# A masked softmax bound by its transfers: the cuts of the stores of batches 6 to 12

## The chip, the cores and the metric

The kernel runs on one core of a Trainium2 chip. The metric is the device time of one execution in microseconds (us); a smaller one is better. Most runs of one kernel agree within about 0.3%. "Faster" or "slower" means by more than 2%. Batches, loads and stores are numbered from 0, so "store 6" writes batch 6, the seventh.

## The reference

```python
x: float32 [16, 8, 256, 256]        # batch, heads, seq_q, seq_k
lengths: int32 [16], each in 128..255
for b in range(16):
    m = x[b, :, :, :lengths[b]]
    e = exp(m - max(m, axis=-1))
    result[b, :, :, :lengths[b]] = e / sum(e, axis=-1)      # the rest of result is 0
```

A batch is 2048 rows of 256 numbers, 2.10 MB. The inputs are drawn with a fixed seed, so the lengths, and with them the bytes that the loads bring, are the same in every run. A load has landed when the engine that waits for it sees all of it arrived, shortly after its last packet. A hole is a stretch in which the DMA engines have too little to do.

## The kernel before

A batch lies in SBUF as 128 partitions of 16 rows (`nt` = 16), each partition 16 KB and contiguous in memory too. There are eight slots. Loads 0 to 3 go out on SyncE's queue; loads 4 to 15 on GpSimd's, each only as wide as its batch's length needs. VectorE masks (one instruction a batch), ScalarE takes exponentials and row sums, VectorE divides (two halves a batch); SyncE stores. The cuts of the stores are in `parts`:

```python
def parts(b):
    if b == 0:
        cuts = [0, nt]
    elif b < 10:
        cuts = [0, half, half + quarter, nt]
    elif b < 12 or b == batch - 1:
        cuts = [0, half, nt]
    else:
        cuts = [0, nt]
    return [slice(i, j) for i, j in zip(cuts, cuts[1:])]
...
# SyncE: the stores
for b in range(batch):
    s_b = s_st[b % 2]
    for s in parts(b):
        nc.sync.wait_ge(s_out, 2 * b + (s.stop - 1) // half + 1)    # the divisions that it needs
        if b >= 2 and s.start == 0:
            nc.sync.wait_ge(s_b, 64 * (b // 2 + 1))                 # store b-2 has landed
        nc.sync.dma_start(out=out_f[b, :, s, :], in_=xt[:, b % slots, s, :]).then_inc(...)
...
# GpSimd: load n waits for load n-2 and for store n-8
# VectorE: the order of its work
for b in range(batch):
    ...
    mask(b + 1); divide(b, 0); divide(b, 1)
```

At most two batches' stores, and two loads, are in flight. A part that ends in the first half needs one division, a whole store needs both. And batch b is divided only after the mask of batch b+1, so it waits for load b+1.

The softmax here doesn't subtract the row's maximum and nothing guards it: scores larger than these inputs give would overflow.

Of the kernel before, what the change touches and what calls it, by code (L numbers as in the profile page):

```python
# [20 lines left out]
def kernel(  # L21
# [9 lines left out]
    batch, heads, seq_q, seq_k = x.shape  # L31
# [18 lines left out]
    def parts(b):  # L50


        if b == 0:
            cuts = [0, nt]
        elif b < 10:
            cuts = [0, half, half + quarter, nt]
        elif b < 12 or b == batch - 1:
            cuts = [0, half, nt]
        else:
            cuts = [0, nt]  # L60
        return [slice(i, j) for i, j in zip(cuts, cuts[1:])]
# [17 lines left out]
    with tc.tile_critical(no_gpsimd_drain=True):  # L79
# [32 lines left out]
# [3 lines that stand above are left out]
                nc.sync.wait_ge(s_out, 2 * b + (s.stop - 1) // half + 1)  # L115
                if b >= 2 and s.start == 0:
                    nc.sync.wait_ge(s_b, 64 * (b // 2 + 1))
                nc.sync.dma_start(  # L118
                    out=out_f[b, :, s, :], in_=xt[:, b % slots, s, :]
                ).then_inc(s_b, 16 * ((s.stop - s.start) // quarter))  # L120
# [162 lines left out]
```

## Time and profile before

The kernel before takes 156.7 us (156.70 to 157.01 in four runs). Its profiled execution took 156.32 us, with a span of 154.7.

| what | before | how it is read |
|---|---|---|
| bytes moved | 62.08 MB | page, DMA queues; the change leaves it as it is |
| DMA share, 24 to 139.5 us | 1.01 to 1.02 | by stretch; the DMA share is the mean busy share of the 16 DMA engines, and about 1.01 is what full engines show in these records |
| mask 14, mask 15 start | 120.01, 127.35 | VectorE in order of time; mask 14 starts when its load has landed; mask 15 when its load has (127.14) and VectorE has ended its division (127.24) |
| last division ends | 139.46 | the same |
| last packet of a store ends | 152.8 | packet records |

The lines themselves stand in the prediction.

### The profile page before, as it was taken

The numbers are of one execution on the slowest core, as the hardware profiler recorded it, in microseconds if no ns is written. First come the engines' busy times: TensorE is split into PE (matmuls) and PEld (weight loads), VectorE is DVE, ScalarE is ACT, GpSimd is POOL, SyncE is SP. The second block draws the span as 40 slices with busy tenths as digits, with TensorE's granted clock in tenths as the row PEclk, the third lists the DMA queues.
The fourth block names the chain that finished last, engine by engine and source line by source line (L and its number), as shares of the span: only waits on it lengthen the run. The fifth ranks groups of instructions, "written<-read, shape, count | busy, mean of one in ns | idle before, by whom it ended". The sixth has DMA issues, their size and how long they took to land.

```text
span 154.7 us, 1317 instructions
## 1 busy us (share of the span) xinstructions
PE 0.2 (0%) x1; PEld 0.1 (0%) x1; DVE 115.1 (74%) x84; ACT 105.2 (68%) x514; POOL 19.0 (12%) x25
## 2 busy tenths in 40 slices
PE   0000000000000000000000000000000000000000
PEld 0000000000000000000000000000000000000000
DVE  1249999952999994966979499999894999990000
ACT  3087799992698997591978849798969297920000
POOL 4910031000320200202020020202000000000000
DMA  4999999999999999999999999999999999999993
GB/s 108 430 445 424 436 309 416 409 411 436 423 404 388 423 405 416 412 412 422 398 421 412 411 413 404 414 409 412 417 409 450 417 420 426 443 432 436 424 415 144
DMA packets 10132, 62.08 MB, mean 401 GB/s; under 512 B 866, under 2 KB 962, under 8 KB 6802
## 3 DMA queue, kind: packets, MB, share of 16 engines
q1 hardware_dynamic: 6048, 41.95, 66.1%
q0 software_dynamic: 4080, 20.12, 32.1%
q14 instruction: 2, 0.02, 0.0%
q10 hardware_dynamic: 2, 0.00, 0.0%
HBM read 28.51 MB, written 33.55 MB: 401 GB/s over the span
## 4 chain that ended last, share of the span: by engine, by line
DMA 71%; DVE 12%; issue 4%; POOLq 1%; SPq 1%; DVEq 0%
DMA xt<-in_x_dram 60%; DMA out_dram<-xt 11%; DVE xt L222 9%; DVE xt L195 3%; SPq L109 1%; POOLq L135 1%; DVE inv_sum L219 0%; POOLq L130 0%; SPq L111 0%; SPq L118 0%; POOLq L157 0%; POOLq L159 0%; DVEq L212 0%; POOLq L137 0%; SPq L278 0%
## 5 line engine op out<-in xcount | busy, mean ns | idle before, releaser
L249 ACT ACTIVATE xt<-xt x256 | 102.4, 402 | 29.6 <-DVE xt L195 29.6
L222 DVE TENSOR_TENSOR xt<-xt,inv_sum 128x2048 f32<-128x2048 f32 x32 | 73.3, 2292 | 1.1
L195 DVE SCALAR_TENSOR_TENSOR xt<-down,len_s,xt 128x2048 f32<-128x2048 f32 (+1 forms) x17 | 37.8, 2224 | 19.8 <-DMA xt<-in_x_dram 19.4
L249 ACT ACTIVATION_READ_ACCUMULATOR xt<-xt x256 | 48.1, 188 | 0.0
L130 POOL DMA_DIRECT2D xt<-in_x_dram x12 | 12.8, 1066 | 91.3 <-DMA out_dram<-xt 62.8
L219 DVE RECIPROCAL inv_sum<-row_sum 128x8 f32<-128x8 f32 x32 | 6.3, 196 | 1.2 <-ACT xt L249 1.2
L149 POOL MEMSET xt<- 128x1536 f32 x4 | 5.3, 1387 | 1.1 <-DVE len_s L186 1.1
L241 ACT ACT_TABLE_LOAD x1 | 1.3, 1283 | 1.6 <-SPq L79 1.6
L178 DVE TENSOR_SCALAR down<-iota_i 128x256 f32<-128x256 int32 x1 | 0.3, 299 | 1.6 <-POOL iota_i L141 1.6
L183 DVE CAST len_b<-word 1x16 bf16<-1x16 int32 x1 | 0.2, 162 | 0.4 <-DMA word<-in_lengths_dram 0.4
L186 DVE TENSOR_SCALAR len_s<-len_f 128x16 f32<-128x16 f32 x1 | 0.2, 175 | 0.3 <-PE len_f L165 0.3
L141 POOL IOTA iota_i<- 128x256 int32 x1 | 0.3, 332 | 0.6 <-SPq L79 0.6
L146 POOL MEMSET seed<- 1x1 f32 x2 | 0.3, 164 | 0.0
L241 ACT ACTIVATE warm<-const-float32-0.0 128x1 f32<-128x1 f32 x1 | 0.2, 203 | 0.0
L144 POOL MEMSET ones<- 1x128 bf16 x1 | 0.2, 197 | 0.0
L165 PE MATMUL len_f<-len_b,ones 1*128 1x16 bf16 x1 | 0.2, 164 | 2.6 <-DVE len_b L183 2.6
L267 POOL MEMSET const-float32-0.0<- 128x1 f32 x1 | 0.1, 99 | 0.3 <-issue 0.3
L165 PEld LDWEIGHTS len_f<-len_b,ones 1*128 1x128 bf16 x1 | 0.1, 99 | 2.6 <-POOL ones L144 2.6
L267 POOL MEMSET const-float32-1.0<- 128x1 f32 x1 | 0.1, 99 | 0.0
L267 POOL MEMSET const-bfloat16-1.0<- 128x1 bf16 x1 | 0.1, 99 | 0.0
L267 POOL MEMSET const-uint8-127<- 128x1 uint8 x1 | 0.1, 99 | 0.0
L267 POOL BASE_LOAD x1 | 0.0, 17 | 0.1
## 6 DMA issues: line engine op xcount, KB each, us to landing
out_dram<-xt SPq DMA_DIRECT2D x15, 1024.0 KB
out_dram<-xt SPq DMA_DIRECT2D x18, 512.0 KB
out_dram<-xt SPq DMA_DIRECT2D x4, 2048.0 KB
xt<-in_x_dram SPq DMA_DIRECT2D x3, 2048.0 KB, 16.1
xt<-in_x_dram POOLq DMA_DIRECT2D x3, 1728.0 KB, 15.9
xt<-in_x_dram POOLq DMA_DIRECT2D x2, 2048.0 KB, 17.5
xt<-in_x_dram POOLq DMA_DIRECT2D x2, 1600.0 KB, 15.1
xt<-in_x_dram POOLq DMA_DIRECT2D x2, 1280.0 KB, 14.2
```

What stands on the lines that cost most here:

```text
L109: nc.sync.dma_start(out=xt[:, 0, s], in_=x_f[0, :, s]).then_inc(s_ld[h], 16)
L130: nc.gpsimd.dma_start(out=xt[:, slot, :, :w], in_=x_n[:, n, :, :w]).then_inc(s_sw[par], 16)
L135: with nc.gpsimd.If(v <= ws[m]):
L141: nc.gpsimd.iota(iota_i, pattern=[[1, seq_k]], base=0, channel_multiplier=0).then_inc(s_iota, 1)
L149: nc.gpsimd.memset(xt[:, b, :, low:], 0.0).then_inc(s_fill, 1)
L165: nc.tensor.matmul(len_f, lhsT=ones, rhs=len_b, start=True, stop=True).then_inc(s_lenf, 1)
L195: return nc.vector.scalar_tensor_tensor(out=t, in0=down[:, None, lo:hi].to_broadcast([P, s.stop - s.start, hi - lo]), scalar=len_s[:, b : ...
L219: step(nc.vector.reciprocal(out=inv_sum[:, b, s], in_=row_sum[:, b, s]))
L222: nc.vector.tensor_tensor(out=t, in0=t, in1=inv_sum[:, b, s, None].to_broadcast([P, half, seq_k]), op=ALU.mult,).then_inc(s_out, 1)
L241: nc.scalar.activation(out=warm, in_=nc.const_aps.tensor(0.0, (P, 1), F32), func=EXP)
L249: ins = nc.scalar.activation(out=e, in_=e, func=EXP, accum_out=sum_h[:, bass.ds(i, 1), j])
L267: nc = _bacc.Bacc("TRN2", target_bir_lowering=False, num_devices=1)
```

## The change

The intent is fewer and larger store transfers (37 become 34) in the part of the run where loads and stores share the engines, with the compute left as it is.

```diff
-        elif b < 10:
+        elif b < 6:
             cuts = [0, half, half + quarter, nt]
-        elif b < 12 or b == batch - 1:
+        elif b < 13 or b == batch - 1:
             cuts = [0, half, nt]
```

Stores 6 to 9 change from a half and two quarters to two halves, store 12 from whole to two halves. The others keep their cuts.

## The prediction

> **What bounds the kernel now.** I read the page from the top, then the stretches by engine, the chain, the waits of SyncE's queue, and the DMA queues stretch by stretch. Batches are numbered from 0. The page of the kernel before says:
>
> ```profile
> span 154.7 us, 1317 instructions
> PE 0.2 (0%) x1; PEld 0.1 (0%) x1; DVE 115.1 (74%) x84; ACT 105.2 (68%) x514; POOL 19.0 (12%) x25
> DMA  4999999999999999999999999999999999999993
> GB/s 108 430 445 424 436 309 416 409 411 436 423 404 388 423 405 416 412 412 422 398 421 412 411 413 404 414 409 412 417 409 450 417 420 426 443 432 436 424 415 144
> DMA 71%; DVE 12%; issue 4%; POOLq 1%; SPq 1%; DVEq 0%
> ```
>
> No compute engine is full, while the DMA engines are over 90% busy in 38 of 40 slices. The chain is 71% DMA. The 62.08 MB that the page counts at about 420 GB/s make nearly the whole span. So only three things can move the time: bytes, cost per byte, or a moment in which the DMA engines have nothing to do. The stretches (last columns: DMA share, GB/s) show that there is none until the stores are drained:
>
> ```profile
> 24.00:80.00 56.00, 0.00 (x0) 0.00 (x0) 45.62 (x32) 44.16 (x220) 5.91 (x6) 1.00 1.01 413
> 80.00:127.10 47.10, 0.00 (x0) 0.00 (x0) 41.88 (x30) 37.08 (x185) 5.17 (x5) 1.00 1.02 416
> 127.10:139.50 12.40, 0.00 (x0) 0.00 (x0) 12.11 (x10) 8.51 (x43) 0.00 (x0) 1.00 1.02 435
> ```
>
> The last piece of the chain and the waits of SyncE's queue from 80 us on show that compute is not what ends the kernel:
>
> ```profile
> 137.17 2.29 DVE xt L222
> ```
>
> ```profile
> SPq L117 <- DMA out_dram<-xt: 62.3, 9, 8.9
> SPq L122 <- DMA out_dram<-xt: 8.2, 1, 8.2
> ...
> SPq L118 <- DVE xt L222: 0.4, 1, 0.4
> ```
>
> The last division ends at 139.5, 15 us ahead of the end; stores wait for stores (at most two batches' stores are in flight), hardly ever for data. Loads too are two deep: the chain is a row of loads, each issued when the one before the last has landed. So both queues always hold work, and how they share the engines depends on the size of their packets. The records of single packets show a whole store as packets of 16384 B, a half as 8192, a quarter as 4096; the loads' packets are 4320 to 4800 B (loads 5 and 15: 16384).
>
> The share is seen by asking for the queues of single stretches (q1 stores, q0 loads; MB; share). Store 6's half, 80.0 to 84.1:
>
> ```profile
> q1 hardware_dynamic: 154, 1.03, 60.6%
> q0 software_dynamic: 156, 0.67, 40.8%
> ```
>
> Its two quarters, 84.1 to 89.4:
>
> ```profile
> q0 software_dynamic: 276, 1.11, 52.5%
> q1 hardware_dynamic: 277, 1.06, 49.7%
> ```
>
> As many packets pass on either side (154 and 156; 277 and 276). For 1.05 MB stored, loads get 0.67 MB beside a half and 1.11 MB beside two quarters.
>
> **What the Trainium skill says.** "DMA: Bandwidth & Descriptors", section "Queues, rings and completion order", says that each DMA engine takes turns between the queues that have work, a packet at a time. The equal counts above agree. The same page, "Bandwidth", gives a fabric ceiling of 435 GB/s; the stretch after the last load moves 435 by the view, and 431 over whole stores by packet times, so stores alone run at it. "VectorE: DVE Perf Modes" gives 2291 ns for an fp32 tensor_tensor of 2048 elements; the row of the division shows 2292, so the compute of the tail won't change.
>
> **The change, part by part.** Stores 1 to 5 keep their cuts. Stores 6 to 9 turn their two quarters into a half; 10 and 11 were halves already; 12 goes from whole to two halves. 13 and 14 stay whole, 15 stays halves. Nothing differs before store 6's second half, at 84.1.
>
> (a) Cost of packets. 8 quarters of 128 packets go (1024 packets of 4096 B, 162.9 ns each by the packet records) and one whole store (128 of 631 ns); 6 halves come (768 of 316.4 ns). −166.9 − 80.8 + 243.0 = −4.7 us of engine time, over 16 engines −0.3 us. Six issues at some 0.45 us fewer on SyncE's queue: off the path, because it mostly waits.
>
> (b) Share of the loads. Six windows at the first halves of stores 4 to 9 gave loads of 0.70, 0.68, 0.67, 0.70, 0.58 and 0.58 MB; mean 0.65 (the low ones hold the end of a load). No second half runs beside these small packets in the trace; single quarters took 0.555 each, with one turn more for each store's closing packet, so I choose 0.59. A store batch of two halves then carries 2.10 + 1.24 = 3.34 MB, at 416 GB/s 8.04 us. Before it carried about 1.8 MB of loads in 9.5 us (79.95 to 89.51 by the packets): close to the mean load of 20.12/12 = 1.68 MB, one load for one store. After, stores run ahead of the loads.
>
> (c) Where loads end. From 80.0 to 127.1 the load queue moves 9.40 MB (the queue's line for that stretch), 2.10 of it load 15, so 7.30 MB are left up to load 14. That takes 7.30/1.24 = 5.89 store batches of 8.04 us: load 14 drains at 127.3 instead of 119.1. Load 15 has big packets and beats halves two to one; it took 7.3 us (119.1 to 126.4) beside some 1.1 MB of stores. After: until 134.6 instead of 126.4, 8 us later.
>
> (d) What stores are left then. At 127.3 store 11 lacks 0.11 of a batch, 0.24 MB. By 134.6, 1.1 MB more are out, so store 12 has 2.10 − 0.86 = 1.24 MB left: 2.9 us at 431 GB/s, until 137.5.
>
> (e) When later stores are ready. VectorE starts a mask about 1.2 us after a load's last packet (14: 0.9, 13: 1.4, 12: 1.3) and ends that turn's second division 7.2 us after (127.35 to 134.58 in the tail: 2.35 + twice 2.45). Mask 14 at 128.5, store 13 ready at 135.7, its packets 1.0 to 1.1 us after the issue (the first load: 1.14 to 2.15), 136.8: in time for 137.5. Store 13 drains 4.87 us later, at 142.4. Mask 15 starts at 135.7 (load 15 and VectorE are both there), so store 14, which is whole and needs both divisions, is ready at 142.9, and its packets start at 144.0. The DMA engines are empty for 144.0 − 142.4 = 1.6 us. Store 15's halves are ready at 145.4 and 147.8, before store 14 is out: no second gap.
>
> Check: at present store 14 is ready at 134.6 but issued at 138.6, and its predecessor drains at 142.8; some 7 us of slack are there, and the loads' 8 us delay uses them up.
>
> Sum: −0.3 + 1.6 = +1.3 us on 156.7: 158.0. An error in (b) makes the gap longer more easily than it makes it vanish, so I put 158.1.
>
> **The rivals.**
> 1. Nothing but bytes: the engines are full anyway, the order is indifferent, and only (a) remains: 156.4. For it: 7 us of slack in the tail, and 0.69 MB in the undisturbed halves. With 1.28 MB a batch, working (c) to (e) again leaves a gap near 1 us, so 157.4; for none at all the loads must get about 1.33.
> 2. Loads starve more: if a second half lets through just 0.50 MB (1.14 a batch), load 14 drains near 129.5, store 13 itself comes late by about 2 us, and store 14 late by another 2 or so: 160.6. For it: the second half is unmeasured. Against it: turns are by packet, and even the poorest half gave 0.58.
> 3. Faster by better streaming: larger packets raise the mixed rate from some 410 (quarters) to 416 (halves). That is the same gain as (a), a quarter of a microsecond; the total can't fall by 2% (3.1 us) without removing bytes.
> 4. The stores run dry earlier, at compute. Store 12 needs load 13, drained at about 115.8 by the same rates, so it is ready at 124.2 against a start near 128. About 4 us are spare; it doesn't bind, and even if it did, the loads would use the engines.
>
> **Range and chances.** Rival 1 sets the low end, 156.4; 1.14 to 1.18 MB a batch sets the high end, 160.0. The limit of 2% above is at 159.8. Faster by over 2%: 1%, since nothing removes 3 us of traffic. Slower by over 2%: 12%, which needs rival 2 nearly whole. Within 2%: 87%.
>
> **What would show it.** To 84 us the traces should match. From there to the last load: two equal halves per store, loads at some 150 GB/s instead of 190, rate 414 to 418. The last load lands near 135.6 instead of 127.1; the last division ends near 147.8 instead of 139.5. SyncE's queue should wait for the division of batch 14, with a hole of 1 to 2.5 us in the DMA row near 142 to 144, and the division (not a store) as the last link before the final stores. The prediction is wrong if loads end before 132 (loads get more per half than I take), if there is no hole, or if there are two (store 13 late too).

## The result, and the profile after

The changed kernel takes 159.17 us (159.11 to 159.46, four runs) against 156.74. The ratio is 1.0155, with a 95% interval of 1.0137 to 1.0172: slower by 1.5%, which counts as the same at the 2% limit but is far outside the noise. Here and below a ratio is the mean time of one kernel's fast runs over that of the other's of the same rounds, so it is not quite the ratio of the medians quoted.

Four rows of the page of the kernel after:

```profile
span 157.6 us, 1314 instructions
PE 0.2 (0%) x1; PEld 0.1 (0%) x1; DVE 115.2 (73%) x84; ACT 105.2 (67%) x514; POOL 19.0 (12%) x25
DMA  4999999999999999999999999999999999894994
GB/s 125 437 428 441 420 308 419 414 407 434 423 404 390 419 411 421 404 417 412 407 419 423 418 412 413 413 419 410 422 420 416 421 442 418 354 403 196 403 399 200
```

The engines' busy times are as before. What is new stands in the DMA row, a slice being 3.94 us: an 8 and a 4 near the end, and in the row below them 354 and 196 GB/s. Over the last ten slices the kernel before didn't fall under 415 until its very last. The stretches around them (from and to, length, busy us and instructions of PE, PEld, VectorE, ScalarE and GpSimd; last three columns: clock, DMA share, GB/s):

```profile
80.00:127.30 47.30, 0.00 (x0) 0.00 (x0) 35.39 (x25) 32.42 (x161) 5.16 (x5) 1.00 1.02 417
...
137.30:138.50 1.20, 0.00 (x0) 0.00 (x0) 1.09 (x2) 1.20 (x7) 0.00 (x0) 1.00 0.61 259
138.50:143.30 4.80, 0.00 (x0) 0.00 (x0) 4.73 (x5) 3.95 (x20) 0.00 (x0) 1.00 0.91 386
143.30:145.80 2.50, 0.00 (x0) 0.00 (x0) 2.47 (x3) 2.50 (x15) 0.00 (x0) 1.00 0.25 105
```

While loads and stores run together the engines stay full, at 417 GB/s, as before. Then they run dry around 138 and again around 144, while VectorE is busy all through. Counted against a full share of 1.01, the idle time is 0.40 × 1.2 + 0.10 × 4.8 + 0.76 × 2.5 = 2.9 us. The spans differ by 157.6 − 154.7 = 2.9 us, so the holes account for the whole loss.

Who waits, from SyncE's queue after 80 us, to be held against the 0.4 us for a division before (us in all, times, longest):

```profile
SPq L117 <- DMA out_dram<-xt: 45.5, 8, 8.4
SPq L118 <- DVE xt L222: 24.2, 9, 7.6
SPq L122 <- DMA out_dram<-xt: 6.0, 1, 6.0
```

Stores now wait nine times, 24.2 us in all, for a division: they have caught up with the compute. The chain says why the division is late (start, us, what):

```profile
120.26 17.00 DMA xt<-in_x_dram
137.29 0.06 DVEq L212
137.35 0.15 issue
137.50 2.35 DVE xt L195
139.85 0.12 DVE inv_sum L219
140.00 2.29 DVE xt L222
142.29 0.12 DVE inv_sum L219
142.44 2.29 DVE xt L222
144.73 0.12 DVE inv_sum L219
```

The last load lands at 137.3 instead of 127.1. The chain names that load, but VectorE was busy with the turn before, of mask 14, until 137.38, and that turn had begun late because load 14 landed late. Mask 14 before and after (in brackets: how long VectorE had been idle, and for what):

```profile
120.01 2.35 DVE L195 SCALAR_TENSOR_TENSOR xt<-down,len_s,xt 128x2048 f32<-128x2048 f32 x1 [2.08 <-DMA xt<-in_x_dram]
```

```profile
130.16 2.35 DVE L195 SCALAR_TENSOR_TENSOR xt<-down,len_s,xt 128x2048 f32<-128x2048 f32 x1 [3.90 <-DMA xt<-in_x_dram]
```

So both loads are late together. The mask and the two divisions after it cost what they did before: the second division ends 7.23 us after the mask's start. Store 14 is whole, so it is issued at 144.75, after the second division, while store 13's packets end at 143.4. And the share while a store's first half (79.4 to 83.4) and second half (83.4 to 87.4) pass, q1 being stores and q0 loads (packets, MB, share):

```profile
q1 hardware_dynamic: 146, 1.04, 62.4%
q0 software_dynamic: 146, 0.63, 39.1%
```

```profile
q1 hardware_dynamic: 145, 1.06, 63.3%
q0 software_dynamic: 144, 0.62, 38.6%
```

Equal packet counts again, 146 and 146, 145 and 144: the loads get 1.25 MB in a batch of two halves, where a half and two quarters gave them 1.78.

### The profile page after: what moved, and what is told of

It reads as the page before. It is cut to its first block, busy times and chain, and to the rows that moved or that the text cites. A ratio compares the mean times of both kernels' runs of the same rounds, so it can differ in the third digit from the quotient of the medians.

```text
span 157.6 us, 1314 instructions
## 1 busy us (share of the span) xinstructions
PE 0.2 (0%) x1; PEld 0.1 (0%) x1; DVE 115.2 (73%) x84; ACT 105.2 (67%) x514; POOL 19.0 (12%) x25
## 4 chain that ended last, share of the span: by engine, by line
DMA 76%; DVE 12%; issue 3%; SPq 2%; POOLq 1%; DVEq 0%
DMA xt<-in_x_dram 55%; DMA out_dram<-xt 21%; DVE xt L222 9%; DVE xt L195 3%; SPq L118 1%; SPq L109 1%; DVE inv_sum L219 0%; POOLq L130 0%; POOLq L135 0%; POOLq L99 0%; SPq L111 0%; POOLq L157 0%; POOLq L153 0%; DVEq L212 0%; POOLq L159 0%
```

## The experiments

The theory: larger store packets leave the loads a smaller share, the loads land late, and store 14, which has to wait for both divisions after the last load, leaves the DMA engines empty. Its rivals are that larger packets or longer mixing make bytes dearer; that each changed store costs something by itself; that batch 12's new cut is part of it; and that the number of transfers, not the size of their packets, sets the share. All twelve runs gave correct results. Diffs are against the changed kernel or the kernel before, as said.

### Halves at the very end

The changed kernel, with 13 and 14 in halves too:

```diff
-        elif b < 13 or b == batch - 1:
-            cuts = [0, half, nt]
         else:
-            cuts = [0, nt]
+            cuts = [0, half, nt]
```

> The changed kernel with batches 13 and 14 stored in two halves as well. Theory (loads come late because halves take the engines from them, and store 14, being whole, waits for both divisions after the last load): the loads still land at about 137, as in the changed kernel, but store 14 can start after its first division, 2.45 us earlier; the holes in the DMA row shrink from about 3.3 us to about 1, and the time is about 156.8 (ratio to before 1.000). Rival (mixing larger store packets with loads costs bandwidth, holes are incidental): stays at 159.

Measured: 156.94 us, ratio 1.0003 (0.9981 to 1.0025). The same with batch 14 alone in halves:

```diff
-        elif b < 13 or b == batch - 1:
+        elif b < 13 or b >= batch - 2:
```

> The changed kernel with batch 14 alone in halves; 13 stays whole. Theory: only the start of store 14 after the last load sets the end, so the first, shorter hole (before store 13) costs nothing more, and the time equals that of the run with both in halves, about 156.8. Rival (both holes add up): between that run and the changed kernel, about 157.8.

Measured: 156.55 us, ratio 0.9985 (0.9954 to 1.0016). Its stretches show that only the first hole is left (300 GB/s) and that the second, which would lie at 143 to 144, is gone:

```profile
137.00:138.20 1.20, 0.00 (x0) 0.00 (x0) 1.09 (x2) 1.20 (x7) 0.00 (x0) 1.00 0.71 300
138.20:143.00 4.80, 0.00 (x0) 0.00 (x0) 4.73 (x5) 3.95 (x20) 0.00 (x0) 1.00 0.94 398
143.00:144.00 1.00, 0.00 (x0) 0.00 (x0) 1.00 (x1) 1.00 (x7) 0.00 (x0) 1.00 1.07 451
```

The last load landed at 137.0, late as ever (136.9 in the run with both in halves). So the late loads alone do no harm. One cut in the tail wins the whole loss back, which brings down the rival of dearer bytes: with the same packets up to the tail, nothing is lost. That the cut is no gain by itself is seen from the last run below: without a hole to close, batch 14 in halves gained nothing (0.9998 against 0.9981). The two runs' intervals overlap. That fits the first hole having no price of its own: with both in halves, store 13 starts earlier, but the engines then wait before store 14 (a share of 0.62 from 141.8 to 143.3).

### One part of the change at a time

The kernel before with batch 12 alone in halves:

```diff
-        elif b < 12 or b == batch - 1:
+        elif b < 13 or b == batch - 1:
```

> The kernel before with batch 12 alone changed from whole to halves. Theory: store 12 runs after the last load there, so its packets take nothing from a load: 156.7, last load landing at 127. Rival (the cut of batch 12 costs part of the loss): above 157.3.

Measured: 157.09 us, ratio 1.001 (0.9982 to 1.0038). The landing came at 128.8, not 127; the time held. The cut can't have caused that: load 14 was already 1.7 us late (landed at 121.4 against 119.8), before store 12 is issued, and at 80 us this execution had 9.65 MB left to load against 9.41. So a landing alone scatters by more than a microsecond from one execution to another.

The kernel before with batches 6 to 9 alone, batch 12 still whole:

```diff
-        elif b < 10:
+        elif b < 6:
             cuts = [0, half, half + quarter, nt]
```

> The kernel before with the quarters of batches 6 to 9 turned into a half, and batch 12 left whole. Theory: these four stores carry the whole delay of loads 10 to 14; and since store 12 then runs beside load 15 with packets as large as the load's, load 15 lands still later than in the changed kernel (about 139.5 instead of 137.3), and the time is 160.5 to 161.5. Rival (the halves of batch 12 are part of the loss): at most 159.

Measured: 160.44 us, ratio 1.0215 (1.0185 to 1.0246), at the edge of what was expected. Its stretches have one hole, longer than the changed kernel's:

```profile
127.30:142.30 15.00, 0.00 (x0) 0.00 (x0) 10.55 (x8) 7.31 (x37) 0.00 (x0) 1.00 0.99 421
142.30:147.00 4.70, 0.00 (x0) 0.00 (x0) 4.63 (x5) 4.70 (x25) 0.00 (x0) 1.00 0.07 28
```

The last load landed at 138.6. The halves of batches 6 to 9 carry the loss. The new cut of batch 12 is no cost: beside late loads it is a help of some 0.6% (1.0215 against 1.0155, in different rounds). Load 15's packets are 16384 B, and with store 12 in halves they meet smaller ones, with store 12 whole packets as large as its own. The landings show it: from load 14's to load 15's are 9.8 us here, and 7.3 in the kernel before, in the changed one and in both runs of the section before. Batch 12's cut as a cause of the loss is thereby out.

### How much delay the tail takes

The kernel before, with only batches 6 and 7 in halves, and with 6, 7 and 8:

```diff
-        elif b < 10:
+        elif b < 10 and b not in (6, 7):          # second run: (6, 7, 8)
```

> The kernel before with the quarters of batches 6 and 7 alone turned into a half. Theory (slack): each such store puts the loads back by about 1.5 us; two put the last load's landing from 127 to about 130, less than the 7 us of slack in the tail, so there is no hole and the time is 156.5 to 156.8. Rival (each larger store costs by itself, a fourth of the loss apiece): 157.9.

> The kernel before with the quarters of batches 6, 7 and 8 turned into a half. Theory (slack): last load at about 132, still inside the slack: 156.4 to 156.9. Rival (a fourth of the loss apiece): 158.5.

Two: 156.40 us, ratio 0.9981 (0.9964 to 0.9997), no loss though two of four stores were changed. So the rival of a price for each store falls here, and the slack stands. But the last load landed at 132.2, not at 130. Three: 158.39 us, ratio 1.0103 (1.0055 to 1.015): a miss for the theory as I had worked it out, and nearer the rival's number. One of its four runs, of 160.19 us, counts as slow and is not in the ratio; the other three spread over 1.2 us, from 157.62 to 158.83, so that the size of this loss is rough. Its trace shows the hole of the theory, though:

```profile
142.20:144.70 2.50, 0.00 (x0) 0.00 (x0) 2.47 (x3) 2.50 (x13) 0.00 (x0) 1.00 0.28 118
```

The last load landed at 136.0, not 132. I had counted only what stores 6 to 8 themselves take from the loads. But when loads fall behind, stores 10 and 11 (halves already) and 12 (whole) come to lie beside loads that used to be over by then; for 10 and 11 that is argued only. For 12 the landings show it again: 9.1 us from load 14's to load 15's, against 7.3 in the run with two. So I put batch 12 in halves there as well:

```diff
-        elif b < 10:
+        elif b < 10 and b not in (6, 7, 8):
...
-        elif b < 12 or b == batch - 1:
+        elif b < 13 or b == batch - 1:
```

> The run with batches 6, 7 and 8 in halves, and batch 12 in halves as well. That run was 1% slow against my expectation of none; its trace shows store 12, whole, beside the end of load 15. Theory A (the whole store 12 takes half the turns by size and puts load 15 back): now the last load lands by 134.5, the hole before store 14 is under 0.6 us, and the time is 156.3 to 156.9. Theory B (three larger stores put the loads back far enough by themselves, with halves 10 and 11 falling beside load 14): a hole of 1 us or more stays and the time is 157.5 or more.

Measured: 156.86 us, ratio 1.0006 (0.9987 to 1.0025). The time is theory A's. The trace is not: the last load landed at 135.4, and from 142.2 to 144.0 the DMA share is 0.43, a hole of 1 us:

```profile
142.20:144.00 1.80, 0.00 (x0) 0.00 (x0) 1.77 (x3) 1.80 (x11) 0.00 (x0) 1.00 0.43 182
```

The profiled execution was the slowest of the six (157.32 us), so it may show more of a hole than most. Its load 14 landed at 128.1, not 126.9 as with store 12 whole, and at 80 us, before the first store that differs from the kernel before had changed anything, it had 9.57 MB left to load against 9.42. From load 14's landing to load 15's were 7.3 us again. So the cut of store 12 did to load 15 what theory A said, 1.8 us sooner, and the late start of this execution hid two thirds of it. The whole store 12 accounts for most of the loss of the run with three; how much hole the others leave in a usual execution was not settled.

### Packet size or number of transfers

The changed kernel, with stores 6 to 12 still two transfers of 1 MB each, but each made of alternate quarters, so that a contiguous piece is 4096 B:

```diff
+            if 6 <= b < 13:
+                nc.sync.wait_ge(s_out, 2 * b + 2)
+                nc.sync.wait_ge(s_b, 64 * (b // 2 + 1))
+                for u in range(2):
+                    nc.sync.dma_start(
+                        out=out_f[b].rearrange("p (i u j) c -> p i u (j c)", i=2, u=2)[:, :, u],
+                        in_=xt[:, b % slots].rearrange("p (i u j) c -> p i u (j c)", i=2, u=2)[:, :, u],
+                    ).then_inc(s_b, 32)
+                continue
             for s in parts(b):
```

> The changed kernel with the same number of store transfers of the same size for batches 6 to 12, two of 1 MB each, but each takes alternate quarters, so that its contiguous pieces are 4096 B and not 8192. Theory (the size of the packets sets the share): the loads get more than before the change, the last lands at or before 127, there are no holes, and the smaller packets cost about 1 us against the changed kernel's streaming: about 157.5. Rival (the number of store transfers, each with its closing packet, sets the share): last load at about 137 and a time of 159 or more.

Measured: 157.47 us, ratio 1.0055 (1.0039 to 1.0072), and the last load landed at 122.6, 14.7 us before the changed kernel's. The queues from 82 to 92 us (stores q1, loads q0):

```profile
q0 software_dynamic: 510, 2.15, 53.7%
q1 hardware_dynamic: 511, 1.96, 49.1%
```

Packet for packet once more, 510 and 511, and now the loads get more than the stores. The number and size of the transfers are the changed kernel's; the pieces differ, and each store here waits for both its divisions, but all were issued at least 2.8 us after the second, so that this wait held none of them. So the size of the packets sets the share. (Where a load ends, counts can be unequal: 37 and 88 from 92 to 93 us; a microsecond before and after they match.) It also costs: the stretch from 122.5 to 136.0, stores alone in 4096-B packets, ran at 410 GB/s, against 431 in the stretch that follows, 136 to 152, most of whose bytes are in larger packets. Summed over all packets of the two queues the engines worked 153.2 us here, 151.8 in the changed kernel and 151.9 in the kernel before. These 1.3 us more are enough for the 0.9 by which this kernel, without a hole, is slower than the one before.

### Halves everywhere

The changed kernel with batches 1 to 5 in halves too:

```diff
-        elif b < 6:
+        elif b < 1:
```

> The changed kernel with batches 1 to 5 in halves too. Theory: the loads fall back further until the stores run dry at compute; the last load lands at 138 or later and the time is 159.5 to 161. Rival (bytes and packet cost alone): faster than the changed kernel by a few tenths, 158.9.

Measured: 159.78 us, ratio 1.021 (1.0186 to 1.0235), within the expected range, but the last load landed at 137.25, where the changed kernel's did (137.26). Load 9's last packets ended 5.5 us later than in the changed kernel (83.7 against 78.2), and by load 14 the difference was gone. The stores' issues show what limits it: from store 8 to store 12 every half was issued within 0.03 us of the end of its own division. Stores that have caught up with the compute stop, and the loads then have the engines: from 101.6 to 103.5 us no packet of a store ran, and the DMA share was 1.02. The delay limits itself.

### Something faster?

The DMA row of the kernel before falls to 309 GB/s in one slice, and to 303 between 20 and 24 us. I let GpSimd's first load start one landing earlier, with batches 6 and 7 in halves and without:

```diff
-        nc.gpsimd.wait_ge(s_ld[ahead - 1], 16)
+        nc.gpsimd.wait_ge(s_ld[ahead - 2], 16)
```

> A try at a faster kernel: the run with batches 6 and 7 in halves, and the first load of the second queue issued one landing earlier (it waits for load 1 instead of load 2). Theory: the DMA row of the kernel before falls to 303 to 309 GB/s between 20 and 24 us because the first queue has run out; an earlier load fills that, worth up to 1.1 us: 155.4 to 155.9. Rival (load 4 then takes from load 3 and what is won at the start is lost by batch 3): 156.4 as without.

> The kernel before with only the earlier issue of load 4. Theory: the same gain as in the run beside it, 155.6 to 156.1. Rival: 156.7.

Measured: 157.00 us, ratio 1.0025 (1.0003 to 1.0047), and 156.76 us, ratio 1.0007 (0.9987 to 1.0026). Both miss. Load 4 was issued at 16 us instead of 20.8, but the stretch stayed as slow; the kernel before and the second run there:

```profile
20.00:24.00 4.00, 0.00 (x0) 0.00 (x0) 3.93 (x5) 4.00 (x21) 1.71 (x2) 1.00 0.97 303
```

```profile
20.00:24.00 4.00, 0.00 (x0) 0.00 (x0) 3.93 (x5) 4.00 (x22) 0.00 (x0) 1.00 0.99 315
```

I should have looked at the share beside the rate: 0.97. The engines were not idle there, their packets took longer for their bytes: in the kernel before 833 ns on average for one of 16384 B, 614 before 20 us. Why, these runs don't show.

Last, whether the 0.998 of the run with batches 6 and 7 is a gain: the same, with batch 14 in halves:

```diff
-        elif b < 10:
+        elif b < 10 and b not in (6, 7):
...
-        elif b < 12 or b == batch - 1:
+        elif b < 12 or b >= batch - 2:
```

> The run with batches 6 and 7 in halves (156.40 us, ratio 0.998) with batch 14 in halves too, to see whether a small gain over the kernel before is real. Theory: no hole was left there, so the cut of batch 14 adds nothing; the small packet saving stays: ratio 0.997 to 0.999. Rival (that ratio was chance, the engines are full either way): 1.000.

Measured: 156.64 us, ratio 0.9998 (0.9981 to 1.0015). No gain is established. None of the versions beats the kernel before by more than its interval and repeatably.

## Why the prediction was right, and where it was off

The prediction was 158.1 us in a range of 156.4 to 160.0, with 87% on "within 2%"; the measurement was 159.17 and within 2%. The mechanism holds: the loads fall behind by their share, store 14 waits for both divisions, the engines run dry. The size was too small: +1.3 us in the working, +2.4 in the timed medians and +2.9 between the profiled spans. And two holes came where one was forecast; two, with store 13 late too, stood among the prediction's own signs of being wrong. The forecast hole of 1.6 us held 1.9; the one before it, with the thin stretch between, added 1.0; and of the 0.3 us of cheaper packets only 0.06 came.

**Packets' cost (a).** Predicted −0.3 us. Summed over all packets of the two queues, the engines' work fell by 0.06 us, from 151.87 to 151.81. I had taken mean durations per size, and the mean of the 16384-B packets (631 ns) holds 74 slow ones from 20 to 24 us (833 ns); those of the tail took 611. Without the one store that went, the mean rose to 637. Two comparisons without a hole, 0.9981 and 0.9998, leave room for 0.3 us or nothing. Small either way.

**The share (b).** Right: 0.65 and 0.59 MB for the two halves were chosen, 0.63 and 0.62 were measured. The Trainium skill's "DMA: Bandwidth & Descriptors", section "Queues, rings and completion order", on which it rests, agrees with the equal counts wherever both queues held work, and the run with alternate quarters shows that the packet is the unit.

**Where the loads end (c).** This is the term that failed. I had load 14 drained at 127.3 and its mask at 128.5; the mask started at 130.16, 1.7 us later. The instant of 127.3 was worked out from bytes, as if the engines finished together, while the 119.1 beside which it stands, and the "about 1.2 us" of step (e), count from a load's last packet. By bytes load 14 was out at 127.7, the time at which the load queue had only load 15's bytes left; its last packet ended at 129.18, 1.5 us after. In the kernel before the same two moments are 118.63 and 119.06, 0.4 us apart. Step (e)'s wait itself held: from the last packet to the mask 0.98 us, against 0.95 before.

Is it an accident of one execution? Three other runs have the same stores up to store 11: the two with a changed tail, and batches 6 to 9 alone. Their load 14 was out by bytes at 128.3, 128.1 and 127.6, its last packet ended at 128.8, 128.9 and 128.4, and mask 14 started at 129.8, 129.9 and 129.1. So the landing comes later than worked out every time, by 0.6 to 1.7 us. But how much of it is bytes (0.3 to 1.0 us) and how much the spread of the engines (0.5 to 1.5) changes from one execution to the next; a spread as wide as 1.5 us was seen in the changed kernel's execution alone of these four. Why the engines come apart was not tested.

**The stores left (d), and the readiness (e).** Store 12 was to drain at 137.5, and the first hole begins at about 137.3. From load 14's delay everything follows as written, that much later: store 13 ready at 137.39 instead of 135.7, too late for store 12's end by about a microsecond (predicted: in time by 0.7); mask 15 at 137.50 instead of 135.7 (load 15, whose 7.3 us after load 14 held, landed at 137.26 and VectorE was free at 137.38: both there together, as forecast); store 14 ready at 144.73 instead of 142.9. The compute took just what was put down for it, 7.23 us from mask to second division. Nearly all of that delay of 1.8 us goes to the end: predicted span 154.7 + 1.3 = 156.0, measured 157.6.

**The rivals.** Rival 1 (only bytes) is wrong: there are holes. Rival 2's shape came (two holes, store 13 late too), though not for its reason, since the second half isn't starved (0.62 MB and not 0.50). Rival 3 is out, with no gain seen. Rival 4 (stores dry at compute) is met in the run with halves everywhere, and there, as it said, the loads use the engines. In the changed kernel it was nearer than worked out: store 12's second half was ready at 126.25, not 124.2.

## What to carry to other kernels

Where two queues share full DMA engines packet by packet, as here, the length of the contiguous pieces acts as a priority: it delayed one stream by 10 us with the total rate the same (416 and 417 GB/s), and the price showed up only where that stream's last transfers had work behind them. Work out the slack at the tail before enlarging anything ahead of it, and count what the delay pushes the late transfers against. When an end is worked out from bytes, add the time until the last engine has finished. A hole may also be closed at the point where it opens: here, cutting one store in the tail so that it can start after half of its data gave the whole loss back.

## What the Trainium skill lacked or had wrong

- "DMA: Bandwidth & Descriptors", "Queues, rings and completion order", tells of turns by packet, but not that a plain store's packet, in the records of these runs, is as long as its contiguous piece, so that the cut sets the share: beside 4096-B, 8192-B and mixed packets a batch of stores let pass about 2.3, 1.25 and 1.78 MB of loads (2.15 × 2.10 / 1.96 for the first). Its section "SWDGE vs HWDGE vs iDMA" calls for packets of at most 4096 B by preference; GpSimd's loads here had packets of 4320 to 4800 B, with a shorter one for what is left over, and its two loads of full width had packets of 16384.
- The same page, "Bandwidth", lets HBM bind at about 358 GB/s for transfers between HBM and SBUF, though its own table has 425 and its note gives the lower figure for both cores of a pair streaming; one core alone here ran at 417 with loads and stores mixed, and at 431 with stores in 16384-B packets. It has no rate for stores by packet size: 4096-B packets alone ran at 410.
- The same page, "Why a DMA increments its semaphore by 16 and not by 1", says that the engines finish independently and that only the full count is safe. It gives no size for it: between the end of load 14's bytes in sum and its last packet lay 0.4 us before the change, and 0.5 to 1.5 in four executions with larger stores, and the waiting engine pays that.
- No page accounts for the stretch from 20 to 24 us, where engines at a share of 0.97 moved 303 GB/s in packets of 833 ns instead of 614, nor do these runs.
